# Row maxima of an 8192 x 8192 matrix on one core: loads of 256 consecutive rows with transposed results, and runs of 48 and 16 rows in place of 46 and 18

## The chip, the core and the metric

The kernel runs on one core of one Trainium2 chip. The metric is the device time of one execution in microseconds (us), as the median over several runs. A core has compute engines that run side by side, each with its own queue of instructions: here VectorE (DVE in the profile) does nearly all the arithmetic, GpSimd (POOL) joins small results, and SyncE (SP) and ScalarE (ACT) only issue DMA transfers. All transfers share the core's 16 DMA engines. Data is computed on in SBUF, an on-chip memory with 128 partitions; input and output lie in HBM.

## The reference

```python
def setup_inputs():
    return {"x": np.random.randn(8192, 8192).astype(np.float32)}

def reference(x):
    return np.linalg.norm(x, ord=np.inf, axis=1)
```

The infinity norm along axis 1 of a matrix that is handled row by row here is the largest absolute value of each row, as `np.linalg.norm` defines it for vectors. The output holds 8192 numbers. The input is 268.4 MB (8192 x 8192 x 4 bytes), each number is read once, and the output is 32 KB.

## The kernel before

A row is 8192 numbers, 32 KiB. The rows are split in two at `split` (L138): the last `ROWS` x 128 = 18 x 128 = 2304 rows are the tail, and the first 5888 rows are the big part.

**The big part** is read by `n_big` = 23 loads of 128 partitions x 16384 numbers (8 MiB). The view `x_big` (L143) gives each partition a run of 46 consecutive rows, and load t takes rows 2t and 2t+1 of every run. So one load takes 64 KiB from each of 128 places, and neighbouring places lie 46 rows, 1472 KiB, apart. One `tensor_reduce` (L110, called from L157) makes from each load two maxima per partition, in `res_big[:, t, :]`. Since a partition's 46 results belong to consecutive rows, one store writes them all (L221, "early").

**The tail** gives each partition a run of 18 rows (`x_tail`, L144), 576 KiB apart. `tail_loads` (L26) cuts these 18 x 8192 numbers of a partition into 29 loads, from the end backwards. It is a planner: with a linear model of the time of a load (`LOAD`, L15) and of a reduction (`REDUCE`, L16) it makes the loads ever smaller, so that each reduction ends about when the next load lands, and only a short reduction stands behind the last load. The first tail load has 16384 numbers per partition, then come 10048, 14528 and three of 8192, and at the end 1152, 1024, 896, 768 and 704. A row that falls into several loads gets partial maxima, which GpSimd combines (L207). The last row's partial maxima are put behind the last load's data in SBUF, so that the last reduction takes them in as well (`behind`, L181).

**Buffers and order.** All loads go into one ring of 3 x 16384 numbers per partition (`Pieces.room`, L82), apart from the last row's, which have places of their own. Every load is issued on SP's queue (L92), in the order of the program. There are five load semaphores (`SEMS`); load i waits until the reduction of load i-5 is done (L98), and for room in the ring. Each reduction waits for its load's semaphore (L120). VectorE takes the reductions in the order of the loads.

**Stores.** ACT issues two: "early" (L221, the 46 results of each partition) and "middle" (L225, 16 of the 18 tail results). Both wait for the third reduction from the end, `pieces.last[-3]` (L231). SP issues the last store (L240, two tail results per partition) behind the last reduction and two tiny `memset`s on VectorE (L218), and then waits for what is still out (the loop at L243).

Of the kernel before, what the change touches and what calls it, by code (L numbers as in the profile page):

```python
# [7 lines left out]
P = 128  # L8
R = 2
RING = 3 * 16384  # L10
APART = 2048
SEMS = 5


LOAD = (1.1775e-3, 0.073)  # L15
REDUCE = (1.0417e-3, 0.060)  # L16
SPARE = 0.08
ROWS = 18
FIRST = 768
SNAP = 0.6  # L20
GRAIN = 64
# [4 lines left out]
def tail_loads(n_cols, big):  # L26

    slack = 0.0
    lag = REDUCE[0] * FIRST + REDUCE[1]
    loads = []
    end = ROWS * n_cols

    def take(top, bottom, most):
        nonlocal slack  # L40
        w = 0
        n = 0
        spare = SPARE if loads else 0
        while True:

            n += 1
            start = max(bottom, (top - 1) // n_cols * n_cols - (n - 1) * n_cols)
            fit = int((lag + slack - spare - REDUCE[1] * n) / REDUCE[0])
            w = max(w, min(fit, top - start) // GRAIN * GRAIN)
            if fit <= top - start or start <= bottom:  # L50
                break
        w = max(GRAIN, min(w, most, top - bottom))
        row = (top - w + n_cols - 1) // n_cols * n_cols
        if top - row >= SNAP * w or (w == most and top > row):
            w = top - row
        n = (top - 1) // n_cols - (top - w) // n_cols + 1
        slack += (LOAD[0] - REDUCE[0]) * w + LOAD[1] - REDUCE[1] * n
        loads.append((top - w, w))
        return top - w

    ends = [take(end, end - n_cols, FIRST), take(end - n_cols, end - 2 * n_cols, n_cols)]
    for top, bottom in zip(ends, (end - n_cols, 0)):
        while top > bottom:
            top = take(top, bottom, big)
    return loads[::-1]


class Pieces:
# [7 lines left out]
    def __init__(self, tc, ring):  # L76
        self.tc, self.nc, self.ring, self.head = tc, tc.nc, ring, 0
        self.sems = [tc.alloc_semaphore(f"loaded{i}") for i in range(SEMS)]
        self.started = self.reduced = 0
# [9 lines left out]
    def load(self, at, w, src):  # L89
        i = self.started  # L90
        self.started += 1
        ins = self.nc.sync.dma_start(out=self.ring[:, at : at + w], in_=src)  # L92
        ins.then_inc(self.sems[i % SEMS], 16)
        self.tc.no_tile_sem_insts.add(ins.ins.name)
        self.tc.declare_no_dep(ins.ins, group="loads", reason="a reduction stands in between")
        self.tc.add_to_no_dep_group("loads", ins.ins)
        if i >= SEMS:
            self.tc.add_manual_dep(  # L98
                ins.ins,
                self.last[i - SEMS].name,  # L100
                mybir.DependencyInfo(mybir.DependencyClass.Sync, mybir.DependencyReason.DATA),
# [3 lines left out]
    def reduce(self, pairs):  # L105
# [3 lines left out]
        for k, (dst, src) in enumerate(pairs):  # L109
# [9 lines left out]
            else:  # L119
                ins.wait_op(self.sems[i % SEMS], 16 * (i // SEMS + 1), "sem-ge")  # L120
            self.tc.declare_no_dep(ins.ins, group="loads", reason="waits on the load's semaphore")
# [4 lines left out]
@with_exitstack  # L126
def kernel(
    ctx: ExitStack,
    tc: tile.TileContext,
    x: bass.AP,  # L130
    out: bass.AP,
):
    nc = tc.nc
    f32 = mybir.dt.float32
    n_rows, n_cols = x.shape

    tail = tail_loads(n_cols, R * n_cols)
    split = n_rows - ROWS * P  # L138
    n_big = split // (R * P)

    x_big = x[:split].rearrange("(p t r) m -> t p (r m)", p=P, r=R)  # L143
    x_tail = x[split:].rearrange("(p r) m -> p (r m)", p=P)  # L144

    single = ctx.enter_context(tc.tile_pool(name="single", bufs=1))
    ring = single.tile([P, RING + APART], f32)
    res_big = single.tile([P, n_big, R], f32)
    res_tail = single.tile([P, ROWS], f32)
    idle = single.tile([1, IDLE], f32)  # L150
    pieces = Pieces(tc, ring)

    for t in range(n_big):
        at = pieces.room(R * n_cols)
        pieces.load(at, R * n_cols, x_big[t])
        buf = ring[:, at : at + R * n_cols]
        pieces.reduce([(res_big[:, t, :], buf.rearrange("p (r m) -> p r m", r=R))])  # L157


    parts = []  # L160
    for i, (start, w) in enumerate(tail):
        c = 0
        while c < w:
            row = (start + c) // n_cols
            n = min(w - c, (row + 1) * n_cols - start - c)
            parts.append((row, i, c, n))
            c += n
    of_row = [[q for q in parts if q[0] == row] for row in range(ROWS)]

    spots, behind, dst = {}, {}, {}
    at = RING
    for row, own in enumerate(of_row):
        if row == ROWS - 1:
            spots[own[-1][1]] = at
            at += own[-1][3]
            for q in own[:-1]:
                dst[q] = ring[:, at : at + 1]
                at += 1  # L180
            behind[own[-1]] = len(own) - 1  # L181
            dst[own[-1]] = res_tail[:, row : row + 1]
        elif len(own) == 1:
            dst[own[0]] = res_tail[:, row : row + 1]
        else:
            some = single.tile([P, len(own)], f32, name=f"parts{row}")
            for k, q in enumerate(own):
                dst[q] = some[:, k : k + 1]
    assert at <= RING + APART and len(behind) == 1
    for i, (start, w) in enumerate(tail):  # L190
        at = spots[i] if i in spots else pieces.room(w)
        pieces.load(at, w, x_tail[:, start : start + w])
        done = pieces.reduce(
            [
                (dst[q], ring[:, at + q[2] : at + q[2] + q[3] + behind.get(q, 0)])
                for q in parts
                if q[1] == i
            ]
        )
        for row in range(ROWS - 1):  # L200
            if len(of_row[row]) > 1 and of_row[row][-1][1] == i:
                best = dst[of_row[row][0]]
                more = [dst[q] for q in of_row[row][1:]]
                while more:
                    two, more = more[:2], more[2:]
                    to = best if more else res_tail[:, row : row + 1]
                    combined = nc.gpsimd.tensor_scalar(  # L207
                        out=to,
                        in0=best,
                        scalar1=two[0],  # L210
                        scalar2=two[1] if len(two) == 2 else None,
                        op0=mybir.AluOpType.max,
                        **(dict(op1=mybir.AluOpType.max) if len(two) == 2 else {}),
                    )
                    tc.add_to_no_dep_group("combined", combined.ins)
    tc.declare_fence(done.ins, group="loads")
    for i in range(IDLE):
        rest = nc.vector.memset(idle[:, i : i + 1], 0.0)  # L218
        tc.keep_in_program_order(rest)

    early = nc.scalar.dma_start(  # L221
        out=out[:split].rearrange("(p q) -> p q", p=P), in_=res_big.rearrange("p t r -> p (t r)")
    )
    out_tail = out[split:].rearrange("(p r) -> p r", p=P)
    middle = nc.scalar.dma_start(  # L225
        out=out_tail[:, : ROWS - 2], in_=res_tail[:, : ROWS - 2]
    )
    for store in (early, middle):
        tc.add_manual_dep(
            store.ins,  # L230
            pieces.last[-3].name,  # L231
            mybir.DependencyInfo(mybir.DependencyClass.Sync, mybir.DependencyReason.DATA),
            reason="not beside the last load",
        )

    seen = nc.sync.keepalive_nop([nc.sync.lower_ap(res_tail[:, ROWS - 2 : ROWS - 1])])
    tc.keep_in_program_order(seen)
    tc.no_tile_sem_insts.add(seen.ins.name)
    tc.add_to_no_dep_group("seen", seen.ins)
    last = nc.sync.dma_start(out=out_tail[:, ROWS - 2 :], in_=res_tail[:, ROWS - 2 :])  # L240
    tc.declare_no_dep(last.ins, group="combined", reason="SyncE has waited for GpSimd")
    tc.declare_fence(last.ins, group="seen")
    for before in (rest, early, middle):  # L243
        gone = nc.sync.keepalive_nop([])
        tc.keep_in_program_order(gone)
        tc.add_manual_dep(
            gone.ins,
            before.ins.name,
            mybir.DependencyInfo(mybir.DependencyClass.Sync, mybir.DependencyReason.DATA),
            reason="done before the last store lands",  # L250
        )
# [28 lines left out]
```

## Time and profile before

| What | Value |
|---|---|
| median of 3 runs | 628.88 us (628.87 to 628.91) |
| the profiled execution's own time | 628.88 us |
| its span, first to last instruction | 627.1 us |
| VectorE busy | 552.1 us, 62 instructions |
| GpSimd busy | 3.2 us, 14 instructions |
| read from HBM, written | 268.44 MB, 0.03 MB |
| mean transfer rate over the span | 428 GB/s |
| loads issued on SP | 52 |

The span is what the profile records between the first and the last instruction. The 1.8 us by which the execution's time exceeds it lie around it. The page lists busy times by engine, 40 equal slices of the span with the busy share of VectorE and of the DMA engines, and the chain of work that ended last; a group of instructions has the line of the helper that made it, so that every reduction stands at L110 and is told apart by the tile it writes (`res_big`, `res_tail`, `parts`, `ring`) and its shape. "Idle before" is time in which the engine waited directly before such an instruction.

### The profile page before, as it was taken

What the parts mean: (1) busy time and instruction counts of PE and PEld (TensorE: products, weight loads), DVE (VectorE), ACT (ScalarE), POOL (GpSimd) and SP (SyncE); (2) the same over time, 40 slices, a digit from 0 to 9 for tenths busy, and PEclk for the clock granted to TensorE, in tenths of its full rate; (3) what the DMA queues carried; (4) which work ended last, traced back from release to release, by engine and by line L of the source; (5) the groups of instructions that cost most, each with busy time, mean ns of one, the idle gap of its engine ahead of it and who ended that gap; (6) DMA issues with size and microseconds to landing.
All of it is one profiled execution on the core that took longest, in us unless ns stands there. A gap on an engine that the chain in (4) does not pass through costs nothing.

```text
span 627.1 us, 175 instructions
## 1 busy us (share of the span) xinstructions
DVE 552.1 (88%) x62; POOL 3.2 (1%) x14
## 2 busy tenths in 40 slices
DVE  0588988889988889888898888988889999999998
POOL 0000000000000000000000000000000000000000
DMA  9999999999999999999999999999999999999997
GB/s 401 410 460 401 468 401 468 401 468 401 468 401 468 401 468 401 468 401 468 401 464 405 451 418 451 418 439 431 422 437 442 404 435 442 430 422 430 426 422 308
DMA packets 7921, 268.48 MB, mean 428 GB/s; under 512 B 1264, under 2 KB 1264, under 8 KB 2416
## 3 DMA queue, kind: packets, MB, share of 16 engines
q1 hardware_dynamic: 7632, 268.44, 99.3%
q10 hardware_dynamic: 288, 0.03, 0.0%
q14 instruction: 1, 0.01, 0.0%
HBM read 268.44 MB, written 0.03 MB: 428 GB/s over the span
## 4 chain that ended last, share of the span: by engine, by line
DMA 57%; DVE 42%; issue 0%; DVEq 0%; SPq 0%
DMA ring<-in_x_dram 57%; DVE res_big L110 22%; DVE parts L110 12%; DVE res_tail L110 7%; DVE ring L110 1%; DVEq L275 0%; SPq L92 0%; DVE idle L218 0%
## 5 line engine op out<-in xcount | busy, mean ns | idle before, releaser
L110 DVE TENSOR_REDUCE res_big<-ring 128x2 f32<-128x16384 f32 x23 | 396.1, 17220 | 69.4 <-DMA ring<-in_x_dram 69.4
L110 DVE TENSOR_REDUCE parts<-ring 128x1 f32<-128x3136 f32 (+18 forms) x22 | 78.5, 3634 | 1.2 <-DMA ring<-in_x_dram 1.2
L110 DVE TENSOR_REDUCE res_tail<-ring 128x1 f32<-128x8192 f32 (+1 forms) x9 | 69.8, 7811 | 2.1 <-DMA ring<-in_x_dram 2.1
L110 DVE TENSOR_REDUCE ring<-ring 128x1 f32<-128x1600 f32 (+5 forms) x6 | 8.3, 1445 | 0.0
L207 POOL TENSOR_SCALAR res_tail<-parts 128x1 f32<-128x1 f32 x9 | 2.7, 296 | 615.6 <-DVE parts L110 615.6
L207 POOL TENSOR_SCALAR parts<-parts 128x1 f32<-128x1 f32 x1 | 0.4, 353 | 5.6 <-DVE parts L110 5.6
L264 POOL MEMSET const-bfloat16-1.0<- 128x1 bf16 x1 | 0.1, 101 | 0.0
L264 POOL MEMSET const-uint8-127<- 128x1 uint8 x1 | 0.1, 101 | 0.0
L264 POOL MEMSET const-float32-0.0<- 128x1 f32 x1 | 0.1, 99 | 0.2 <-issue 0.2
L264 POOL MEMSET const-float32-1.0<- 128x1 f32 x1 | 0.1, 98 | 0.0
L218 DVE MEMSET idle<- 1x1 f32 x2 | 0.1, 59 | 0.0
## 6 DMA issues: line engine op xcount, KB each, us to landing
ring<-in_x_dram SPq DMA_DIRECT2D x3, 4096.0 KB, 40.5
ring<-in_x_dram SPq DMA_DIRECT2D x1, 7264.0 KB, 31.1
ring<-in_x_dram SPq DMA_DIRECT2D x1, 5024.0 KB, 33.3
ring<-in_x_dram SPq DMA_DIRECT2D x1, 4544.0 KB, 34.6
ring<-in_x_dram SPq DMA_DIRECT2D x1, 4224.0 KB, 40.3
ring<-in_x_dram SPq DMA_DIRECT2D x1, 4032.0 KB, 35.5
ring<-in_x_dram SPq DMA_DIRECT2D x1, 3584.0 KB, 35.4
ring<-in_x_dram SPq DMA_DIRECT2D x2, 1568.0 KB, 18.3
```

What stands on the lines that cost most here:

```text
L110: ins = self.nc.vector.tensor_reduce(out=dst, in_=src, axis=mybir.AxisListType.X, op=mybir.AluOpType.max, apply_absolute_value=True,)
L207: combined = nc.gpsimd.tensor_scalar(out=to, in0=best, scalar1=two[0], scalar2=two[1] if len(two) == 2 else None, op0=mybir.AluOpType.max, ...
L218: rest = nc.vector.memset(idle[:, i : i + 1], 0.0)
L264: nc = _bacc.Bacc("TRN2", target_bir_lowering=False, num_devices=1)
```

## The change

`ROWS` becomes 16, so the tail is 2048 rows and the big part 6144 rows, 24 loads. The view of the big part changes from `(p t r)` to `(t p r)`: load t now takes rows 256t to 256t+255, partition p its rows 256t+2p and 256t+2p+1. One load is one piece of 8 MiB of the input. Its 128 places of 64 KiB are neighbours, 64 KiB apart. In the tail, a partition's run has 16 rows, 512 KiB.

A partition's results of different loads now belong to rows that lie 256 apart. `res_big` is padded to 32 loads (a `memset` on VectorE fills the columns that no load writes), and two transposes on VectorE, one for each of the two rows, turn blocks of 32 partitions x 32 loads; into `lines`, whose partitions are then loads. Four stores on ACT write `lines`, one for each block of 32 partitions, 24 partitions x 64 numbers each. They wait for the ninth reduction from the end in place of the third; "middle" still waits for the third and writes 14 columns in place of 16. SP waits at the end for six things in place of three.

The list of loads stays 52 long with the same widths in the same order: the 16384 numbers that opened the tail are now the 24th big load. On VectorE two reductions of 8192 numbers in `res_tail` become one big reduction of 16384. The transposes stand behind the first reduction of the tail (8192 numbers) and ahead of the second part of the same load (1856 numbers).

```diff
-ROWS = 18
+ROWS = 16
...
-    x_big = x[:split].rearrange("(p t r) m -> t p (r m)", p=P, r=R)
+    x_big = x[:split].rearrange("(t p r) m -> t p (r m)", p=P, r=R)
     x_tail = x[split:].rearrange("(p r) m -> p (r m)", p=P)
...
-    res_big = single.tile([P, n_big, R], f32)
+    res_big = single.tile([P, B, R], f32)
+    lines = single.tile([P, B, R], f32)
...
+    nc.vector.memset(res_big[:, n_big:, :], 0.0)
...
+    for r in range(R):
+        tc.keep_in_program_order(nc.vector.transpose(out=lines[:, :, r], in_=res_big[:, :, r]))
...
-    early = nc.scalar.dma_start(
-        out=out[:split].rearrange("(p q) -> p q", p=P), in_=res_big.rearrange("p t r -> p (t r)")
-    )
+    early = []
+    out_big = out[:split].rearrange("(t q j) -> q t j", q=P // B, j=B * R)
+    for q in range(P // B):
+        of_q = lines[q * B : q * B + n_big].rearrange("t p r -> t (p r)")
+        early.append(nc.scalar.dma_start(out=out_big[q], in_=of_q))
...
-    for store in (early, middle):
+    for store, after in [(x, -9) for x in early] + [(middle, -3)]:
         tc.add_manual_dep(
             store.ins,
-            pieces.last[-3].name,
+            pieces.last[after].name,
...
-    for before in (rest, early, middle):
+    for before in (rest, *early, middle):
```

`B` is 32.

More of the change, by code (lines that the diff above doesn't have):

```diff
@@ L11 @@
 APART = 2048
+B = 32
 SEMS = 5
```

## The prediction

> **What bounds the kernel now.** I read the page's slices first, then the chain, then the groups, then the timeline at the end, and last the DMA view. The page shows two engines that matter:
>
> ```profile
> DVE  0588988889988889888898888988889999999998
> DMA  9999999999999999999999999999999999999997
> ...
> DMA ring<-in_x_dram 57%; DVE res_big L110 22%; DVE parts L110 12%; DVE res_tail L110 7%; DVE ring L110 1%; DVEq L275 0%; SPq L92 0%; DVE idle L218 0%
> ...
> L110 DVE TENSOR_REDUCE res_big<-ring 128x2 f32<-128x16384 f32 x23 | 396.1, 17220 | 69.4 <-DMA ring<-in_x_dram 69.4
> L110 DVE TENSOR_REDUCE parts<-ring 128x1 f32<-128x3136 f32 (+18 forms) x22 | 78.5, 3634 | 1.2 <-DMA ring<-in_x_dram 1.2
> ```
>
> The DMA engines are at 9 tenths or more in every slice but the last. VectorE is not: in the big part a reduction takes 17.22 us and waits for a load each time, 69.4 us in all. From the timeline, with start, duration and what was waited for:
>
> ```profile
> 22.50 17.22 DVE L110 TENSOR_REDUCE res_big<-ring 128x2 f32<-128x16384 f32 x1 [22.50 <-DMA ring<-in_x_dram]
> 41.85 17.22 DVE L110 TENSOR_REDUCE res_big<-ring 128x2 f32<-128x16384 f32 x1 [2.13 <-DMA ring<-in_x_dram]
> ...
> 467.62 25.87 DVE L110 TENSOR_REDUCE res_tail<-ring 128x1 f32<-128x8192 f32 x3 [2.13 <-DMA ring<-in_x_dram]
> 493.41 2.08 DVE L110 TENSOR_REDUCE parts<-ring 128x1 f32<-128x1856 f32 x1
> 496.68 6.75 DVE L110 TENSOR_REDUCE parts<-ring 128x1 f32<-128x6336 f32 x1 [1.20 <-DMA ring<-in_x_dram]
> ```
>
> A load every 41.85 - 22.50 = 19.35 us is 8.39 MB / 19.35 us = 433.5 GB/s. From 496.68 on VectorE never waits, so the chain blames it; yet the loads run just ahead of it. The last load shows that, in the timeline and in the DMA view (issue size, then us to landing):
>
> ```profile
> 619.88 0.33 SPq L92 DMA_DIRECT2D ring<-in_x_dram  x1
> 624.01 0.89 DVE L110 TENSOR_REDUCE res_tail<-ring 128x1 f32<-128x710 f32 x1
> 624.92 0.35 SPq L240 DMA_DIRECT2D out_dram<-res_tail  x1
> ```
>
> ```profile
> ring<-in_x_dram SPq DMA_DIRECT2D x1, 352.0 KB, 4.1
> out_dram<-res_big ACTq DMA_DIRECT2D x1, 23.0 KB, 1.6
> out_dram<-res_tail ACTq DMA_DIRECT2D x1, 8.0 KB, 2.1
> ```
>
> 619.88 + 4.1 = 623.98, and its reduction starts at 624.01: there is no cover. The trace's semaphore events say the same of each of the last dozen loads: landing and start of the reduction lie 0.02 to 0.14 us apart. So whatever makes the stream of loads longer appears whole at the end, although the chain names VectorE there; whatever VectorE saves appears nowhere.
>
> **The pace of a transfer.** The trace's packet records say what sets the stream's pace. A packet is one partition's run: 65,536 bytes in a big load. After the start they take 2.415 to 2.440 us each, big part (1472 KiB pitch) and tail (576 KiB pitch) alike; 32,768 bytes take 1.217. So a packet is 1.203 us for each 32 KiB plus some 0.014 us. Eight of them per DMA engine are 8 x 2.419 = 19.35, the period of a load: there is no gap to remove. Only the first 16 packets, one per DMA engine and all begun between 1.71 and 2.66 us, are slower: 2.53 to 3.40, mean 3.06.
>
> **The change, part by part.** The sum is made against the profiled execution: 628.88 us, span 627.1, 1.8 around it; the median of the runs is the same 628.88.
>
> *Loads.* 52 before and 52 after, same widths, same order, same queue, same waits. Only the addresses change.
>
> *Big loads, 24 of 64 KiB pitch.* No row shows this pitch. Nearest rows: 2.42 us for the two odd pitches (23 x 64 KiB and 9 x 64 KiB). From below: if all 0.014 us beside the bytes vanished, 24 x 8 x 0.014 = 2.7 us, and if the first packets fell to 2.42, 0.64 more: -3.3. From above: 3.06 for every packet would be 24 x 19.35 x 0.64/2.42 = +123. I take 0, since both rows that differ in pitch stand at one value.
>
> *Tail loads, 512 KiB pitch.* They fill 467.60 to 623.98, 156.4 us. Before, neighbouring places differ by 9 x 64 KiB, so they agree only in address bits below 64 KiB. After, all 128 places of a load lie at exact multiples of 2^19 bytes and agree in 19 bits. The DMA engines also walk in step: their 16 parts of a load land within 0.46 to 0.57 us of each other from first to last. If memory is shared out by the lower bits, they now ask for the same places. No row shows the price. Below: -0.014 x 8 x 28 = -3.1, if the packets' overhead vanished. Above: the slow row for every packet, 156.4 x 0.64/2.42 = +41. The 2.42 row is nearer than the 3.06 row, since an engine that is in stride keeps a read ahead. I take one packet in eight at 3.06, the first that each engine begins in a load, when all 16 set out together as at the start: 0.64/8/2.42 = 3.3% of 156.4 = **+5.2**. This is the choice on which the forecast rests.
>
> The page "DMA: Bandwidth & Descriptors" of the Trainium skill, section "Latency and other measured facts", has a row against this change: copies of 128-partition tiles with a row pitch of 512 KiB ran at 207 GB/s per direction where a padded pitch gave 214, and with 2 MiB at 164. By 214/207 the tail would take 3.4% longer, an estimate of +5.3 us; by the trace's 2.42 us row, which only odd pitches show, nothing. Those were copies in both directions, this is reading alone, and no run here shows it yet.
>
> *Transposes and memset on VectorE.* The memset falls into the 22.50 us before the first load lands. Two transposes of 128x32 have no row: above the 0.06 of the 1x1 memset, below the 0.41 of the 256-number reduction, so 0.12 to 0.82 together. They stand ahead of the 1856-number reduction at 493.41, which is followed by 1.20 us of waiting for a load. Even 0.82 leaves 0.38. Queued behind them is only that reduction; SP's next loads wait for it, but a load issued there lands 35 us later, so its queue is full. Cost 0. Without this cover it would still be 0.82 at most, and only if it stood after 496.68. One 17.22 us reduction for two of 8.68 saves 0.1 and ends in the same wait.
>
> *Stores.* One store of 128 packets of 184 bytes is taken from the end, at 623.27. It delays nothing there: its packets begin at 624.14, after the last load, so its removal gains 0. "Middle" is issued 0.4 earlier, at 623.27, and its packets still begin near 624.2. The four new stores follow the ninth reduction from the end, which ends at 615.03. At 0.37 to 0.44 us an issue they go out until 616.7, and their packets run at about 616 to 618, beside loads that have no cover. The 184-byte packets took 0.0147 us and the 64-byte ones 0.0105, so 256 bytes are about 0.017 (an estimate from these). 96 packets and four completions (0.009 each): evenly on 16 engines 6 x 0.017 + 4 x 0.009 = 0.14; all on one engine 1.7. Not less than 0: nothing of them was there before. The stores before were spread over the engines, so I take 0.14, rounded to **+0.15**. The three more waits of SP at the end (a semaphore instruction is 0.021) lie under the 1.4 us of the last store.
>
> Sum: 628.88 + 5.2 + 0.15 = **634.2**.
>
> **The rivals.**
> 1. *The pitch is free.* The DMA engines' own pace stays the limit, and only the four stores remain: 628.88 + 0.15 = 629.0, between 628.6 and 630.1. For it: all packets in stride are within 0.5% of each other at two pitches. Against it: both pitches are odd multiples of 64 KiB, so this trace never tried the case.
> 2. *Faster: consecutive rows read better.* The place is the first packets and the 0.014 us of each packet in the 24 big loads. Its price is at most the -3.3 above, 625.6 plus 0.15. It decides from 1.26 us (0.2%) of net gain on, which is 1.4 of that, over 40% of everything that isn't bytes. Against it: packets are set by bytes almost alone.
> 3. *The big loads lose as well.* 16 engines then work inside one 8 MiB piece. With the same 3.3%: 24 x 19.35 x 0.033 = 15.3 more, 649.5. Against it: 128 consecutive places of 64 KiB cover all values of the bits between 64 KiB and 8 MiB.
> 4. *The change doesn't do what it says*: the stores sit on few engines, or move behind the loads. At most +1.7, 630.6.
>
> **How the numbers follow.** Gains are capped by 3.3 us while losses are capped by nothing near, and the tail has no cover; that makes slower the likelier side. Forecast (tail pitch, 631 to 642 of its own) 0.50; pitch free 0.33; big loads as well 0.07; stores alone over 0.2% 0.04; faster 0.06. A difference under 0.2% (1.26 us) is about what a measurement of this kernel can't tell from no change. Slower: 0.50 + 0.07 + 0.04 = 0.61; same 0.33; faster 0.06. The range runs from 628.5, below the free pitch, to 642; it leaves out rivals 2 and 3 and a little of the forecast's upper end, up to its bound of +41.
>
> **What would show it.** If right: big loads still 19.35 us apart and landing near 467.6, then VectorE waiting for loads in the tail, with packets of 32 KiB above 1.217 us and the tail some 161.6 us long. The two transposes stand between 493 and 496.7 with no new wait. The stores' packets lie near 616 to 618 and shift the last landing by under 0.2. If the tail's packets keep their times, the forecast is wrong and rival 1 right. If the spacing of big loads differs from 19.35, rival 2 or 3 is.

## The result and the profile after

The changed kernel takes 630.0 us (median of 22 runs, 629.58 to 630.52), the kernel before 628.87 us (22 runs, 628.74 to 629.16). The ratio is 1.0018, with a 95% interval of 1.0013 to 1.0024: a loss of 1.1 us that stands clear of noise, and lies just under 0.2%. The forecast was 634.2. The profiled execution took 630.08 us with a span of 628.3, so the span grew by the 1.2 us that the time grew by.

The page of the changed kernel, its slices, its chain and its groups:

```profile
DVE  0588988889988889888898888998889999999998
DMA  9999999999999999999999999999999999999997
...
DMA ring<-in_x_dram 61%; DVE res_big L111 22%; DVE parts L111 9%; DVE res_tail L111 7%; DVE ring L111 0%; DVEq L283 0%; SPq L93 0%; DVE idle L224 0%
...
L111 DVE TENSOR_REDUCE res_big<-ring 128x2 f32<-128x16384 f32 x24 | 413.3, 17220 | 70.9 <-DMA ring<-in_x_dram 70.9
L111 DVE TENSOR_REDUCE parts<-ring 128x1 f32<-128x3136 f32 (+18 forms) x22 | 78.6, 3634 | 1.6 <-DMA ring<-in_x_dram 1.6
...
L164 DVE STREAM_TRANSPOSE lines<-res_big 128x32 f32<-128x32 f32 x2 | 0.3, 189 | 0.0
```

The slices are those of before but for one digit of VectorE; a tail some 3% slower, as forecast, would not show in digits this coarse. The chain gives 4% more of the span to loads (61% in place of 57%), and the partial maxima now wait for loads 1.6 us in place of 1.2. The timeline says where (start, duration, instruction, idle time ahead of it):

```profile
22.53 17.22 DVE L111 TENSOR_REDUCE res_big<-ring 128x2 f32<-128x16384 f32 x1 [21.67 <-DMA ring<-in_x_dram]
...
467.85 17.22 DVE L111 TENSOR_REDUCE res_big<-ring 128x2 f32<-128x16384 f32 x1 [2.13 <-DMA ring<-in_x_dram]
484.98 8.68 DVE L111 TENSOR_REDUCE res_tail<-ring 128x1 f32<-128x8192 f32 x1
493.57 0.30 DVE L164 STREAM_TRANSPOSE lines<-res_big 128x32 f32<-128x32 f32 x2
493.79 2.05 DVE L111 TENSOR_REDUCE parts<-ring 128x1 f32<-128x1856 f32 x1
496.91 6.75 DVE L111 TENSOR_REDUCE parts<-ring 128x1 f32<-128x6336 f32 x1 [1.08 <-DMA ring<-in_x_dram]
...
590.24 4.55 DVE L111 TENSOR_REDUCE parts<-ring 128x1 f32<-128x4224 f32 x1 [0.34 <-DMA ring<-in_x_dram]
595.00 20.99 DVE L111 TENSOR_REDUCE parts<-ring 128x1 f32<-128x3968 f32 x8 [0.20 <-DMA ring<-in_x_dram]
...
616.02 1.77 ACTq L231 DMA_DIRECT2D out_dram<-lines  x4
...
625.19 0.88 DVE L111 TENSOR_REDUCE res_tail<-ring 128x1 f32<-128x710 f32 x1
```

Up to 496.91 only 0.23 us are lost (496.68 before). The two transposes took 0.30 us and ended under the wait, as costed. Then one load comes late, that of 4224 numbers: two waits that weren't there before, 0.34 and 0.20 us. In the kernel before, the five reductions of this stretch stand in one line without a wait:

```profile
578.21 20.12 DVE L110 TENSOR_REDUCE parts<-ring 128x1 f32<-128x2560 f32 x5
```

The DMA views of before and after show that load (2112 KB) 0.7 us slower from issue to landing, 24.4 and 25.1:

```profile
ring<-in_x_dram SPq DMA_DIRECT2D x1, 2112.0 KB, 24.4
```

```profile
ring<-in_x_dram SPq DMA_DIRECT2D x1, 2112.0 KB, 25.1
```

In the packet records one of that load's 128 packets, begun at 588.46, took 1.29 us; the others took 0.63 or 0.64. What ran just ahead of it shows in the DMA view of 587 to 590 us, where queue q14, named "instruction", moves one packet. Queue, kind, packets, MB and share:

```profile
q1 hardware_dynamic: 93, 1.26, 99.8%
q14 instruction: 1, 0.01, 0.7%
```

The kernel before has such a packet too, but in another place, 624 to 625.5 us, where only the stores (q10) are left:

```profile
q10 hardware_dynamic: 288, 0.03, 14.6%
q14 instruction: 1, 0.01, 2.0%
```

By the packet records it is 8192 bytes, begun at 588.14 after (for 0.33 us, up to the start of the slow packet) and at 624.45 before, 0.5 us behind the last load's landing. From the semaphore events the loss grows like this: the last of the 24 loads of 16384 numbers lands 0.23 us later than before, the load of 5056 numbers 0.19, that of 4224 0.97, that of 1024 (with the stores' packets beside it) 1.19, and the last one 0.98. The last reduction still starts 1.18 us later, since VectorE had no cover to take back what that load of 1024 had cost.

### The profile page after: what moved, and what is told of

It reads as the page before. It is cut to its first block, busy times and chain, and to the rows that moved or that the text cites. A ratio compares the mean times of both kernels' runs of the same rounds, so it can differ in the third digit from the quotient of the medians.

```text
span 628.3 us, 183 instructions
## 1 busy us (share of the span) xinstructions
DVE 552.6 (88%) x64; POOL 3.2 (1%) x14
## 4 chain that ended last, share of the span: by engine, by line
DMA 61%; DVE 38%; DVEq 0%; issue 0%; SPq 0%
DMA ring<-in_x_dram 61%; DVE res_big L111 22%; DVE parts L111 9%; DVE res_tail L111 7%; DVE ring L111 0%; DVEq L283 0%; SPq L93 0%; DVE idle L224 0%
## 5 line engine op out<-in xcount | busy, mean ns | idle before, releaser
L111 DVE TENSOR_REDUCE res_big<-ring 128x2 f32<-128x16384 f32 x24 | 413.3, 17220 | 70.9 <-DMA ring<-in_x_dram 70.9
L111 DVE TENSOR_REDUCE res_tail<-ring 128x1 f32<-128x8192 f32 (+1 forms) x7 | 52.6, 7562 | 0.0
```

Source lines behind the costliest of these rows:

```text
L111: ins = self.nc.vector.tensor_reduce(out=dst, in_=src, axis=mybir.AxisListType.X, op=mybir.AluOpType.max, apply_absolute_value=True,)
```

## The experiments

All were timed in five rounds beside the kernel before, 11 runs each (four for runs of 64 rows). The kernel before read 628.80 to 628.85 in them.

### One part of the change at a time

**The big view alone.**

```diff
-    x_big = x[:split].rearrange("(p t r) m -> t p (r m)", p=P, r=R)
+    x_big = x[:split].rearrange("(t p r) m -> t p (r m)", p=P, r=R)
```

> The kernel before with the big view of the change alone (loads of 256 consecutive rows, runs of 46 as 23 such loads; tail of 18 rows, stores as before). Computation: the big results are stored in the order of before, so they stand at other rows; nothing else differs. In the changed kernel's profile the 24th load landed 0.23 us later than before, with most of it lost between the second and the fifth load. Theory 'the pitch of the big loads costs': +0.2 to +0.4 us, near 629.15, with slow packets in the first five loads again. Theory 'the tail's pitch costs' and theory 'the stores cost': no difference, 628.9 within 0.1.

Measured: 629.01 us (628.94 to 629.63), ratio 1.0005 (0.9996 to 1.0014). 0.16 us, inside its interval. In the profile the first load landed at 22.66 in place of 22.47, and from there every big load came 19.35 us after the other; by the last load 0.04 us of it were left. No slow packet followed, against the expectation. The start isn't shown to be the view's: a kernel below with the places of before (the transposes ahead of all reductions) landed its first load at 22.66 too.

**The tail's pitch alone**, the step that the forecast rested on.

```diff
     x_tail = x[split:].rearrange("(p r) m -> p (r m)", p=P)
+    pitch = 16 * n_cols
+    x_tail = bass.AP(tensor=x_tail.tensor, offset=x_tail.offset, ap=[[pitch, P], [1, ROWS * n_cols]])
```

> The kernel before with only the tail's places moved to a distance of 512 KiB: still 18 rows of each place, so neighbouring places overlap by two rows and the last 254 rows are not read; same bytes, same loads. Theory 'the tail's pitch costs' (one packet of the changed kernel's load of 4224 numbers took 1.29 us in place of 0.63, and 0.75 us were lost there): +0.5 to +0.9 us, near 629.6, and a wider spread of the times. Theories 'stores' and 'big pitch': no difference, 628.9 within 0.1. My prediction's price for this step was +5.2, 634.1.

Measured: 628.87 us (628.66 to 629.08), before 628.85; ratio 1.0001 (0.9992 to 1.0009). In the view of waits the partial maxima have the one wait of before:

```profile
DVE parts L110 <- DMA ring<-in_x_dram: 1.2, 1, 1.2
```

The distance of 512 KiB costs this stream in stride nothing. Both my price and the smaller one that I had read into the slow packet are refuted.

**Four early stores alone.**

```diff
...
-    early = nc.scalar.dma_start(
-        out=out[:split].rearrange("(p q) -> p q", p=P), in_=res_big.rearrange("p t r -> p (t r)")
-    )
+    early = []
+    n_line = 24 * 61
+    for q in range(4):
+        early.append(
+            nc.scalar.dma_start(
+                out=out[q * n_line : (q + 1) * n_line].rearrange("(p j) -> p j", j=61),
+                in_=lines[32 * q : 32 * q + 24, :61],
+            )
+        )
...
+    for store, after in [(x, -9) for x in early] + [(middle, -3)]:
...
```

> The kernel before with its early store replaced by four stores of 24 partitions x 61 numbers that wait for the ninth reduction from the end, as in the change. They write zeros from a tile of their own, and the last 32 rows of the big part are not written. Theory 'stores beside loads without cover': +0.15 to +0.3 us, near 629.1, with packets of about 0.02 us between the loads and the loads of 1152 and 1024 numbers landing late. Theories on the pitches: no difference.

Measured: 628.99 us (628.80 to 629.24), ratio 1.0003 (0.9994 to 1.0012). 0.14 us, the size expected, inside its interval. The load of 1152 numbers landed 0.19 us late and the next made most of it good.

**The change without its early stores** (the lines that issue them are taken out).

> The changed kernel without its four early stores, so the big part's results are not written; transposes stay. Theory 'stores': it falls by 0.15 to 0.3 us from the changed kernel's 630.0, to near 629.8. If the stores were the whole difference it would fall to 628.9. If only the pitches matter it stays at 630.0.

Measured: 629.73 us (629.57 to 629.88). The stores are worth 0.27 us here, less than these single comparisons can tell apart. 0.88 us remain, and the slow packet with them: the instruction packet at 588.0, and again one packet of the load of 4224 numbers with 0.66 us too much. A delay that repeats to the nanosecond in two programs (1.292 us in both) isn't a chance collision in memory, and the tail's pitch alone doesn't make it. So my second theory fell too, and the instruction packet became the suspect.

### What brings the instruction packet forward

**Two more tiny instructions at the end of VectorE's program.**

```diff
-IDLE = 2
+IDLE = 4
```

> The kernel before with four in place of two of its tiny memsets on VectorE behind the last reduction, so VectorE has 64 instructions on the page as the changed kernel has, in place of 62. In all profiles so far the queue named 'instruction' moves one 8 KB packet within the span: at 624.45 in the kernel before, when the last load has landed, and at 588.14 in the changed kernel, beside the load of 4224 numbers, of which one packet then took 1.29 us in place of 0.63. Theory 'instruction fetch' (two more instructions on VectorE make the fetch come earlier): the packet moves to near 588, one load packet there loses 0.65 us, and the time goes up by 0.6 to 0.8 us to near 629.55, though the added work is 0.12 us at the very end and nothing else of the change is in. Theory 'addresses' (the slow packet comes from the change's places in memory): no difference beyond 0.1, near 628.95, and the packet stays at 624.4.

Measured: 628.79 us (628.73 to 629.01), before 628.80; packet at 624.34. The plain count of VectorE's instructions isn't it.

**The change with one tiny instruction fewer at the end** (`IDLE = 1`), and **the same with the stores behind the 22nd reduction from the end** (`(x, -22)`).

> The changed kernel with one tiny memset at the end in place of two: 63 instructions on VectorE. Theory 'instruction fetch': the packet goes back to near 624, the load of 4224 numbers lands without delay, and the time falls by 0.6 to 0.8 us to near 629.3; what is left over the kernel before is the stores (0.14 to 0.27) and the big loads (0.16). Theory 'addresses': it stays at 630.0.

> The same, and the four early stores wait for the 22nd reduction from the end in place of the ninth, where VectorE is microseconds behind the loads, so that a load that lands 0.2 us late for a moment delays no reduction. Theory 'the stores' cost is a passing delay that VectorE, without cover at the end, hands on': another 0.15 to 0.25 us less than with one memset alone, near 629.05. Theory 'the stores' packets lengthen the stream of loads for good': no difference between the two.

Measured: 630.11 us (629.69 to 630.50), packet at 588.29; and 629.90 (629.53 to 630.41), packet at 589.00. The count is refuted from this side as well. The earlier stores gave 0.2 us here, within the spread of both. VectorE was not microseconds behind the loads there, as the expectation has it: beside the stores' packets (561.0 to 569.5 us) one reduction started 0.08 us behind its load's landing, and only the next 0.90 behind.

**Transposes added to the kernel before**, at the change's place and, in a second kernel, ahead of all reductions.

```diff
-    res_big = single.tile([P, n_big, R], f32)
+    res_big = single.tile([P, 32, R], f32)
+    lines = single.tile([P, 32, R], f32)
...
+    nc.vector.memset(res_big[:, n_big:, :], 0.0)
...
+    for r in range(R):
+        tc.keep_in_program_order(nc.vector.transpose(out=lines[:, :, r], in_=res_big[:, :, r]))
...
```

> The kernel before with the change's two transposes and its padded res_big added behind the 23 big reductions; what they write is not read, loads and stores are those of before. So far the 'instruction' packet moved in the tail, near 588, in all four kernels with transposes, and at 624 or later in the five others, among them one with as many VectorE instructions as the change. Theory 'transposes bring the fetch forward': the packet moves to the tail of the loads, one load packet beside it takes 0.65 us longer, and the time rises by 0.6 to 0.8 us to near 629.55. Theory 'the 16-row tail brings it' (another program for VectorE): no difference, 628.85. As plain work the transposes cost nothing: 0.4 us under 1.2 us of waiting.

> The kernel before with two such transposes of a tile of zeros ahead of all reductions, under the 22 us in which VectorE waits for the first load; what they write is not read. Theory 'transposes bring the fetch forward, by a table or code that is fetched when they are used': the packet comes soon after the start, or at the same delay of some 95 us behind them, and the loss stays 0.6 to 0.8 us (629.5), since a delay of one DMA engine is kept to the end. If the fetch belongs to a place in the program, it moves by a few instructions and stays near 588. If transposes are not the cause: 628.85.

Measured: 629.50 us (629.36 to 629.70) and 629.55 us (629.31 to 629.79), +0.66 and +0.71; packets at 581.98 and 581.88, and in both one packet of the load of 5056 numbers with 0.66 us too much. The transposes bring the packet, but not where they stand: 490 us of distance between them moved it by 0.1.

**The change with plain copies in place of the transposes** (`tensor_copy`; the big results are stored in another order).

> The changed kernel with its two transposes replaced by two plain copies of the same 128x32 elements, so that the big part's results are stored in a wrong order; count and place of the instructions, loads and stores are those of the change. Theory 'transposes bring the fetch forward': the packet goes back to near 624.5 and the time falls by 0.6 to 0.8 us to near 629.3, which leaves 0.15 to 0.27 for the stores and 0.16 for the big loads. If the fetch belongs to the other parts of the change: 630.0.

Measured: 630.07 us (629.68 to 630.24), packet at 588.16. So it isn't the transpose as an operation: a copy in its place does the same.

**Runs of 48 and 16 rows alone** (`ROWS = 16`, nothing else).

> The kernel before with ROWS = 16 and nothing else: runs of 48 rows for the big loads (places 1536 KiB apart) and 16 for the tail (512 KiB). Theory 'transposes': the packet stays at 624.5; with the pitches free it is 628.9. Theory 'the 16-row tail brings the fetch forward': packet near 588 and 629.55. Runs of 64 rows (2 MiB) cost 22 us in this study, 512 KiB in the tail nothing; 1536 KiB is an odd multiple of 512 KiB and I expect at most 0.5 us of it.

Measured: 629.48 us (629.25 to 629.58), ratio 1.0009 (1.0000 to 1.0018); packet at 625.00, after the loads. So the 16-row tail doesn't bring it. The 0.64 us are more than I expected, and in the profile they are a start: the first load landed at 23.15 in place of 22.47, 0.68 us late. The first load of the tail was 0.57 us late and the last load 0.51, so this tail, 512 KiB apart and without overlap, lost nothing either.

What all of them have in common came from counting. In each early case the packet begins after the 47th recorded instruction of VectorE, small ones and waits included, has started, and before the 48th does. VectorE takes a semaphore wait on its own ahead of its last reduction (at 623.27 in the kernel before). That wait is the 62nd recorded instruction there, the 63rd with one instruction added, and the 64th or later in the early cases. So a theory: VectorE takes in instructions some 17 ahead of the one that runs; on taking in the 64th it fetches the next 8 KB; a wait that stands in front of that place holds the fetch until it ends. The late profiles say the same of the wait: in all nine the packet begins 1.17 to 1.23 us behind this wait's record. In eight that is 0.5 to 0.65 us behind the last load's landing, but in the kernel with runs of 64 rows (below) 0.29 us ahead of it, so the packet follows the wait and not the end of the loads.

**Two, and eight, tiny instructions ahead of all reductions** in the kernel before.

```diff
     pieces = Pieces(tc, ring)
+    for i in range(2):
+        tc.keep_in_program_order(nc.vector.memset(idle[:, :1], 0.0))
```

> The kernel before with two tiny memsets on VectorE ahead of all reductions (0.1 us under a wait of 22), nothing else. Theory 'place in VectorE's program': VectorE fetches the next 8 KB of its instructions when it has taken in a fixed number of them, and it takes them in some 17 ahead of the one that runs, unless a semaphore wait holds it; in the kernel before the wait ahead of the last reduction stands just in front of that place, so the fetch comes when the loads are over. Two more in front push the wait past the place: the packet moves to 588, beside the load of 4224 numbers, and the time rises by 0.6 to 0.7 us to near 629.5. Theory 'only transposes or copies do it': 628.85.

> The same with eight. Theory 'place in VectorE's program': the packet again begins after the 47th recorded instruction of VectorE, which is now six reductions earlier than with two, near 549 to 558, and the cost is the same, near 629.5. Theory 'a fixed time or a fixed load': the packet stays near 588. Theory 'only transposes or copies': 628.85.

Measured: 629.60 us (629.42 to 629.75), ratio 1.0012 (1.0003 to 1.0020), and 629.50 us (629.36 to 629.81), ratio 1.0010 (1.0001 to 1.0019). Packets at 587.76 and 561.03, both after the start of the 47th recorded instruction; the second lies 3 us behind the stretch that the expectation gave, but the count holds. The timelines show the new wait for the load of 4224 numbers with two and, the place being six instructions earlier, for the load of 7168 with eight:

```profile
572.15 17.39 DVE L110 TENSOR_REDUCE parts<-ring 128x1 f32<-128x5632 f32 x4
589.86 4.55 DVE L110 TENSOR_REDUCE parts<-ring 128x1 f32<-128x4224 f32 x1 [0.32 <-DMA ring<-in_x_dram]
594.60 7.61 DVE L110 TENSOR_REDUCE parts<-ring 128x1 f32<-128x3968 f32 x2 [0.19 <-DMA ring<-in_x_dram]
```

```profile
547.02 18.19 DVE L110 TENSOR_REDUCE parts<-ring 128x1 f32<-128x7936 f32 x4
565.69 13.54 DVE L110 TENSOR_REDUCE parts<-ring 128x1 f32<-128x7168 f32 x2 [0.48 <-DMA ring<-in_x_dram]
```

The first of them is the changed kernel's delay, made by 0.1 us of empty work under a wait of 22 us.

**The change with one transpose instruction for both rows.**

```diff
-    for r in range(R):
-        tc.keep_in_program_order(nc.vector.transpose(out=lines[:, :, r], in_=res_big[:, :, r]))
+    tc.keep_in_program_order(
+        nc.vector.transpose(
+            out=lines.rearrange("p b r -> p r b"), in_=res_big.rearrange("p t r -> p r t")
+        )
+    )
```

> The changed kernel with its two transposes of 128x32 made by one instruction of 128x2x32, so one VectorE instruction fewer ahead of the wait; the rest is the change. Theory 'place in VectorE's program': the wait is again in front of the place, the packet goes back to 0.5 us behind the last load, near 624.6, and the time falls by 0.6 to 0.7 us from 630.05 to near 629.35. Theory 'transposes or copies do it': packet near 588 and 630.0.

> The same, with the four early stores behind the 22nd reduction from the end in place of the ninth. Theory 'the stores' cost is a passing delay of loads without cover': another 0.15 to 0.2 us, near 629.15; what is left to the kernel before (0.2 to 0.3) is the start of the big loads. If the stores lengthen the stream for good: 629.35.

Measured: 629.09 us (628.86 to 629.86), ratio 1.0005 (0.9996 to 1.0013): 0.9 of the 1.1 us are gone with one instruction, a little more than expected. The DMA view of 624 to 625.5 us has the packet behind the loads again (624.79):

```profile
q10 hardware_dynamic: 144, 0.01, 6.2%
q14 instruction: 1, 0.01, 1.7%
```

In the view of waits, with us, times and the longest, only the wait of before is left to the partial maxima:

```profile
DVE parts L111 <- DMA ring<-in_x_dram: 1.1, 1, 1.1
```

The second form, with earlier stores, took 629.06 us (628.87 to 629.67). Its profile shows no late load at the end, but 0.03 us are too few to say that the place of the stores matters. No version here beats the kernel before.

### Does a power of two ever cost?

**Runs of 64 rows**: all places 2 MiB apart, in both parts.

```diff
-    x_big = x[:split].rearrange("(p t r) m -> t p (r m)", p=P, r=R)
-    x_tail = x[split:].rearrange("(p r) m -> p (r m)", p=P)
+    n_run = n_rows // P
+    x_runs = x.rearrange("(p r) m -> p (r m)", p=P)
+    x_big = [x_runs[:, t * R * n_cols : (t + 1) * R * n_cols] for t in range(n_big)]
+    x_tail = x_runs[:, (n_run - ROWS) * n_cols :]
...
```

> The kernel before with runs of 64 rows per partition through both parts (46 for the big loads, 18 for the tail): neighbouring places of every load lie 2 MiB apart, so that they agree in 21 address bits. Same loads, same sizes; the two stores go to the rows that belong to them. If power-of-two distances cost a reading stream anything on this chip, it shows here: by the page 'DMA: Bandwidth & Descriptors' of the Trainium skill (164 in place of 214 GB/s at 2 MiB) it would be some 30% longer, near 815. By the 512 KiB run of this study, which cost nothing (628.87), it stays at 628.9.

Measured: 650.94 us (649.87 to 651.99), ratio 1.0352 (1.0338 to 1.0366). It costs, though about an eighth of what I worked out from the Trainium skill's page. The profile's rate by slice shows where:

```profile
GB/s 340 372 429 417 421 429 445 429 429 437 433 437 429 433 437 429 445 425 433 437 433 437 429 433 433 429 445 433 425 431 423 431 438 428 427 427 417 372 240 160
```

Not in the middle. The first four loads lose 7 us; then the DMA engines have spread out (the parts of a load land over 3.7 us in place of 0.46) and the stream runs at full pace, one load every 19.35 us. It loses again at the end: the load of 4224 numbers lands 7.5 us late, the last one 21.0. The loads there have packets of 16 KB and less; which of their properties costs the time was not tried on its own.

## Why the prediction was wrong

1. **The tail loads' pitch, +5.2, is the step that failed.** I took one packet in eight at the 3.06 us of the start. With the pitch alone changed, the runs showed 0.0 (628.87 to 628.85), and the packet records agree: the 384 packets of 32 KiB took 1.213 to 1.225 us there, 1.213 to 1.226 in the changed kernel and 1.213 to 1.227 before, so none was slow. The rival "the pitch is free" had the right mechanism for the loads, and its row (2.42 us at two pitches) was the one to follow. My ground for leaving it, that 16 engines walk in step, was true and cost nothing at 512 KiB: the parts of each tail load landed within 0.55 to 0.64 us of each other in that run. At 2 MiB it did cost: the first four loads lost 7 us until the engines had spread out, and the end of the tail some 14.
2. **Nobody's term: the instruction packet.** 0.65 to 0.75 us (memsets, transposes), of the 1.1. With the packet back behind the loads, the loss that was left (629.09) lay inside the noise, so that the forecast's direction came out is luck. The kernel before had shown it, as one line in the list of DMA queues, and I didn't ask when it came. I costed the added VectorE instructions by their duration and by the wait that covers them, correctly, and not by their place in the program.
3. **The stores, +0.15, fit**: 0.14 alone and 0.27 in the changed kernel, neither clear of noise. Their packets ran at 619.3 to 621.4 us, not at 616 to 618, the first 3.2 us behind its issue at 616.02. The upper bound of 1.7 wasn't reached. That a passing delay isn't given back, since VectorE has no cover, is as the prediction put it.
4. **The big loads, 0, are not refuted**: 0.16 alone, inside the noise. The 0.23 us that the changed kernel's profile had lost by its 24th load came up in the first five loads. They aren't shown to be the pitch's: the profile of the view alone was 0.12 late at its last big load, and that with eight tiny instructions, whose places are those of before, lost 0.41 in its first ten loads. The rival that reads faster is refuted: packets in stride take 2.42 us at 64 KiB too.
5. **The transposes at 0 held as work** (0.30 us under 1.2 of waiting), and so did the padding and the changed waits at the end.

Added up: 0.65 to 0.75 for the packet, 0.14 to 0.27 for the stores, 0.16 for the big loads, 0.95 to 1.18 of the 1.13. The last two are within the noise of a single comparison each; the first is not.

## What to carry to other kernels

Where the DMA engines are full to the end and the arithmetic has no cover, everything that uses them counts, also what the program doesn't issue: look up in the list of queues when instructions are fetched, and count added instructions by place as well as by time. Here a bytes-bound stream in stride kept its pace at every pitch that was tried, so a pitch was to be priced by its start and, at 2 MiB, by the loads of short packets, not by all its bytes. A price taken from the one slow row of a profile needs a reason why that row's condition comes back.

## What the runs showed of the hardware

- VectorE's program brings an 8 KB packet through the DMA engines in the middle of a run. In the nine early profiles it took 0.33 us of one DMA engine, and the load packet behind it 0.66 us more (0.65 once), together some 0.98 us on that engine; the load as a whole, whose last part decides, landed 0.57 to 0.78 us later. The start of the packet lay 0.8 to 4.4 us behind that of the 47th recorded instruction. That VectorE takes in instructions some 17 ahead is worked out from counts in nine early and nine late profiles and from the three predictions that came true; it wasn't seen directly. Two early packets come within 0.8 and 1.0 us of the 47th instruction's start, less than the 1.2 us behind the wait in the late ones, so it can be 18, and what sets the delay within an instruction stays open.
- The page "Runtime: NRT & Kernel Launch" of the Trainium skill, section "Instruction fetch mechanics", says that a sequencer fetches its next block by DMA while the current one runs, at a cost that is mostly hidden. The page has blocks of 16 KiB; the packet here has 8192 bytes. VectorE's new waits are all for loads: it was the stream of loads that lost time by the fetch.
- The start of a stream differed at two pitches: the first load landed at 23.15 us (1536 KiB) and 25.94 (2 MiB), in single profiles, against 22.39 to 22.66 in the sixteen profiles with 1472 or 64 KiB. Between these two no difference is shown.
- The row of the page "DMA: Bandwidth & Descriptors" that the prediction weighed does not carry over to this reading stream: a tail at 512 KiB cost 0.0%, and 2 MiB throughout 3.5%, where the page has copies at 164 in place of 214 GB/s.
